# A decoder trunk on one core: the second MLP product of two chunk-layers by seven products for eight

## The chip, the cores and the metric

The kernel runs on one core of one Trainium2 chip, as one program. The metric is the device time of one execution in microseconds (us). Three runs of the kernel before took 2446.13 us in the median (2443.51 to 2448.79). TensorE multiplies matrices out of SBUF into PSUM, VectorE (DVE) and ScalarE (ACT) work on either, GpSimd (POOL) on SBUF alone, and SyncE (SP) issues most of the transfers.

## The reference

A trunk of two layers works on x, 1024 tokens by 1024 channels, in fp32. Layer 0 mixes tokens by a gated short convolution, layer 1 by sparse attention with three branches; both attend to 256 memory tokens as well, and both end with the same kind of MLP, the part that changes:

```python
x = x + jnp.concatenate([y_tok, y_mem], axis=-1) @ w_out[layer]
hm = rmsnorm(x, mlp_norm[layer])
x = x + jnp.square(jax.nn.relu(hm @ w_up[layer])) @ w_down[layer]
```

`w_up` is 1024 x 4096 and `w_down` 4096 x 1024. After layer 0 the keys and values of layer 1 are built from x.

## The kernel before

Everything is kept transposed: 128 channels on the partitions, tokens along the free dimension. The tokens are cut into two chunks c of 512 (`CH`), so there are four chunk-layers (c, l), worked in the order (0,0), (1,0), (0,1), (1,1). Attention of a chunk is woven between the MLP units of the other; (0,0) and (1,1) have none beside them, except that (0,0) carries the setup of the bias tables and the norms of its neighbours.

An fp32 product is taken as three matmuls in a rounded format (`three`, L266): both operands are split into a high part H (ScalarE copies with rounding, L263) and a low part L (VectorE subtracts, L264), and HH, HL and LH are summed in one PSUM bank. Activations are the moving operand of 512 columns, weights the stationary one of 128x128.

The MLP runs over four blocks b of 1024 hidden channels (`mlp_units`). In a block there are eight up units (`up_unit`), each giving 128 hidden channels: two weight loads of 128x512, 24 matmuls, then ReLU (ScalarE), the square (VectorE for l = 1; for l = 0 a scaling on VectorE and the square on ScalarE) and the split into H and L. Then eight down units (`down_unit`), each adding 24 matmuls to one of the eight tiles of x: one bank, and one VectorE addition of 128x512 from PSUM into x at the end (L1174). In block 3 the finished tile is also written to DRAM.

Weights come through `w_get(n)`: it splits units n to n+2 (`WB` = 3 buffers of H, of L and of the raw weights) and issues the loads of n+3 and n+4 on SP. Three PSUM banks (`mm`) are shared by these units.

The order of the program comes from two planners. The kernel's own (`Issue`) runs generators as threads against an estimated clock and so sets the order of emission: the list `plan` is the main thread, `start` adds others. The tile framework then arranges each engine's queue by its own estimate of when an instruction is ready, allots the buffers of each tag and puts in the waits; an engine works its queue strictly in that order.

Around the change: `bias_setup` starts after the first block's up units of (0,0); the norm of chunk 1 (`a_norm`) starts before the last block's up units; its scaling (`x_scale`, h at L437 and pL at L264) can begin when the last up unit has left its buffers, and the unit after the MLP (`qmem_wide`) needs all of it. `x_apart` loads chunk 1's x into the buffers of tags ks and kw for the last chunk-layer.

Of the kernel before, what the change touches and what calls it, by code (L numbers as in the profile page):

```python
# [29 lines left out]
P3 = [8, 0, 0, 0, 0, 1, 1, 0, 1, 0, 1, 1, 0, 4]  # L30
NTAIL = 6
NWARM = 2
AHEAD = 1
PACE = 2.5
LGM = 0.3
# [110 lines left out]
def trunk(ctx: ExitStack, tc: tile.TileContext, a, out):  # L146
# [7 lines left out]
    def home(tag):  # L154

        return lo if tag in ("ks", "kw", "qs", "ptH", "ptL") else sb
# [114 lines left out]

    units, dma_done, split_done = [], {}, {}

    def w_dma(n):
        if n < len(units) and n not in dma_done:
            t = sb.tile([128, 512], F32, name="wraw", tag="wraw", bufs=WB)
            if len(units[n].shape) == 3:
                DMA.dma_start(t.rearrange("p (t c) -> p t c", c=128), units[n])
            else:
                t = t[:, :units[n].shape[1]]  # L280
                DMA.dma_start(t, units[n])
            dma_done[n] = (t, iss.now + 3.5)

    def w_split(n):
        if n < len(units) and n not in split_done:
            w_dma(n)
            H = lo.tile([128, 512], F32R, name="wH", tag="wH", bufs=WB)
            L = lo.tile([128, 512], F32R, name="wL", tag="wL", bufs=WB)
            raw, t = dma_done[n]
            w = raw.shape[1]  # L290
            H, L = H[:, :w], L[:, :w]
            split(raw, H, L)
            split_done[n] = (H, L, chain(("A", ac(w)), ("V", vc(w)), at=t))

    def w_get(n, cols=128):

        for i in range(n, n + WB):
            w_split(i)
        w_dma(n + WB)
        w_dma(n + WB + 1)  # L300
        H, L, t = split_done[n]
        yield t
        return [x.rearrange("p (k c) -> p k c", c=cols) for x in (H, L)]
# [187 lines left out]
        return chain(("A", ac(256)), ("V", vc(256)))  # L491


    def bias_setup():
        tab = consts.tile([33, 12], F32, name="tab")
        DMA.dma_start(tab, a["table"])
# [2 lines left out]
        for j in range(NRV // 512):  # L499
            oh = lo.tile([33, 512], F32, name="oh", tag="ptH", bufs=PT)  # L500
            DMA.dma_start(oh, a["onehot"][:, 512 * j:512 * (j + 1)])
            yield iss.now + 4
            ohr = lo.tile([33, 512], F32R, name="ohr", tag="ptL", bufs=PT)
            ACT.activation(ohr, oh, AF.Copy)
            yield chain(("A", ac(512)))
            ps = yield from lgb.get()
            for i in range(2):
                PE.matmul(ps[:12, :], tabs[:, i], ohr, start=(i == 0), stop=(i == 1))
            iss.pe(0.43)
            rvs = sb.tile([12, 512], F32, name="rvs", tag="tmp", bufs=TM)  # L510
            ACT.activation(rvs, ps[:12, :], AF.Copy)
            lgb.put(chain(("A", ac(512))))
            DMA.dma_start(rvd[:, 512 * j:512 * (j + 1)], rvs)
        yield iss.now + 5
        for h in range(12):
            dst = skd[h][0:128 * (WP + 1)].rearrange("(p w) -> p w", w=WP + 1)[:, :WP]
# [630 lines left out]
    def up_unit(c, l, j, n):  # L1147
# [20 lines left out]
            As[:] = [None] * KT  # L1168
        yield from dense(n, Hs["m", c], evac, True)

    def down_unit(c, t, last, n):
        def evac(ps):
            x = X[c][t][0]
            V.tensor_tensor(x, ps, x, op=OP.add)  # L1174
            X[c][t][1] = chain(("V", vc(CH)))
            X[c][t][2] += 1
            if last is not None:
                DMA.dma_start(last(t), x)
            return X[c][t][1]
        yield from dense(n, As, evac)  # L1180
# [222 lines left out]
    def x_apart():  # L1403

        yield lambda: Qs[1][KT - 1] is not None
        for tag in ("ks", "kw"):
            x = home(tag).tile([128, 4, CH], F32, name="x2", tag=tag, bufs=1)
            for j in range(4):
                DMA.dma_start(x[:, j], xsd[1][len(X[1])])
                X[1].append([x[:, j], iss.now + 4, 0])  # L1410

# [10 lines left out]
    def mlp_units(c, l):  # L1422
        m = []
        for b in range(4):
            for j in range(8):
                unit(m, up_unit, c, l, j, w=[a["wu"][l, 8 * b + j]])
            last = None
            if b == 3:
                last = (lambda t: xsd[c][t]) if l == 0 else (lambda t: out[c, t])
            for t in range(8):  # L1430
                unit(m, down_unit, c, t, last, w=[a["wd"][l, b, t]])
        return m
# [132 lines left out]

    start(plan, ya, 0)
    start(plan, m_norm, 0, 0)
    plan += out_units(0, 0, x_here)
    m = mlp_units(0, 0)
    plan += m[:8]  # L1570
    start(plan, bias_setup)
    plan += m[8:-16]
    start(plan, a_norm, 1, again(lambda k: a["xT"][1, k]))
    plan += m[-16:-8]
    do(plan, lambda: p_free.add(1))
    start(plan, b_norm, 0)
    plan += m[-8:]


    unit(plan, qmem_wide, fmq[1], w=[(a["am_w"], 512)])  # L1580
# [49 lines left out]
    for fn, args, w in plan:  # L1630
        ns = []
        for x in w:
            ns.append(len(units))
            x, step = x if isinstance(x, tuple) else (x, 512)
            units += [x] if len(x.shape) == 3 else [x[:, i:i + step] for i in range(0, x.shape[1], step)]
        items.append((fn, args + tuple(ns)))

    def main():
# [111 lines left out]
```

## Time and profile before

| | |
|---|---|
| median of three runs | 2446.13 us |
| the profiled execution | 2445.52 us |
| its span, first to last instruction | 2443.8 us |
| granted TensorE clock, mean | 0.997 |
| GpSimd busy over the span | 231.7 us (9%) |
| ScalarE busy over the span | 1287.7 us (53%) |

The span begins with the first instruction; what lies between it and the execution's time is launch and end. A busy time counts the stretch in which an engine has at least one instruction in flight, so pipelined matmuls, whose records overlap, don't add up to it. A row of a group of instructions has the line, engine, operation, tiles and shape, the count, the busy time and the mean duration, and then the idle time before them and what ended it. A row of the timeline has start, duration, engine, line, operation, tiles and shape, and in brackets the idle time that came before.

### The profile page before, as it was taken

The page shows a single profiled execution, that of the slowest core. Times are in us where ns is not written, and L with a number is a line of the kernel's source. Part 1 is how long each engine was busy: PE and PEld are TensorE (multiplying, and loading weights), DVE is VectorE, ACT ScalarE, POOL GpSimd, SP SyncE. Part 2 cuts the span into 40 slices and gives each one's busy share as a digit, 9 for nine tenths or more (in the row PEclk, how much of TensorE's full clock was granted, in tenths as well). Part 3 has the DMA queues.
Part 4 walks back from the last instruction along what each step waited for, and adds up shares of the span by engine and source line. Part 5 has one row for each costly group of instructions (what it writes and reads, how often), then busy time and mean ns, then how long its engine had stood idle before and what let it go on. Part 6 is the DMA issues. An engine that isn't in the chain of part 4 may idle for free.

```text
span 2443.8 us, 35752 instructions
## 1 busy us (share of the span) xinstructions
PE 2414.5 (99%) x12062; PEld 2030.6 (83%) x12062; DVE 1508.8 (62%) x3445; ACT 1287.7 (53%) x2720; POOL 231.7 (9%) x354
## 2 busy tenths in 40 slices
PE   9999999999999999999999999999999999999999
PEld 7878788888888888888888788888888888888887
DVE  6665344464757557777746764788878874644443
ACT  5454343354645537777744553677767763423332
POOL 1120000001100132111110022200010010000000
PEclk9999999999999999999999999999999999999999
DMA  6572553445554565354265558533253244333233
GB/s 179 152 219 95 184 162 95 130 135 154 162 166 132 158 193 128 102 127 103 87 189 190 176 158 218 138 89 87 70 129 90 76 150 137 103 97 98 97 96 107
DMA packets 212791, 327.25 MB, mean 134 GB/s; under 512 B 30211, under 2 KB 79045, under 8 KB 212224
## 3 DMA queue, kind: packets, MB, share of 16 engines
q1 hardware_dynamic: 185664, 287.97, 38.5%
q0 software_dynamic: 26944, 37.00, 7.4%
q8 instruction: 95, 1.56, 0.3%
q14 instruction: 88, 0.72, 0.1%
HBM read 282.63 MB, written 46.38 MB: 135 GB/s over the span
## 4 chain that ended last, share of the span: by engine, by line
PE 85%; DMA 4%; DVE 2%; ACT 1%; issue 1%; POOL 1%; SPq 0%; ACTq 0%; DVEq 0%; POOLq 0%
PE mm L267 23%; PE mm L269 23%; PE mm L268 22%; PE pv L942 5%; PE tr L926 4%; PE lg L842 2%; PE lg L843 2%; PE lg L269 1%; PE lg L268 1%; PE lg L267 1%; DMA wraw<-in_wd_dram 1%; DMA mv<-ev 1%; DVE wL L264 1%; ACT wH L263 0%; POOL r L618 0%
## 5 line engine op out<-in xcount | busy, mean ns | idle before, releaser
L263 ACT ACTIVATE wH<-wraw 128x512 fp32r<-128x512 f32 (+2 forms) x776 | 481.6, 622 | 787.2 <-PE mm L268 594.7
L264 DVE TENSOR_TENSOR wL<-wraw,wH 128x512 fp32r<-128x512 f32 (+2 forms) x776 | 525.6, 679 | 446.0 <-ACT wH L263 433.0
L267 PE MATMUL mm<-pH,wH 128*128 128x512 f32 x1448 | 575.4, 398 | 2.6 <-DVE raw L463 2.1
L268 PE MATMUL mm<-pL,wH 128*128 128x512 f32 x1448 | 566.1, 391 | 1.0 <-DMA pL<-yd 0.8
L269 PE MATMUL mm<-pH,wL 128*128 128x512 f32 x1448 | 566.5, 391 | 0.6 <-DVE wL L264 0.4
L267 PE MATMUL mm<-qH,wH 128*128 128x512 f32 x1152 | 458.4, 398 | 2.7 <-ACT wH L263 2.7
L269 PE MATMUL mm<-qH,wL 128*128 128x512 f32 x1152 | 450.4, 391 | 1.2 <-DVE wL L264 1.1
L268 PE MATMUL mm<-qL,wH 128*128 128x512 f32 x1152 | 449.3, 390 | 0.0
L269 PEld LDWEIGHTS mm<-pH,wL 128*128 128x128 f32 x1448 | 272.6, 188 | 61.0 <-DVE wL L264 3.3
L267 PEld LDWEIGHTS mm<-pH,wH 128*128 128x128 f32 x1448 | 273.1, 189 | 57.7 <-ACT wH L263 3.5
L268 PEld LDWEIGHTS mm<-pL,wH 128*128 128x128 f32 x1448 | 273.3, 189 | 51.8 <-DMA pL<-yd 1.3
L269 PEld LDWEIGHTS mm<-qH,wL 128*128 128x128 f32 x1152 | 216.2, 188 | 50.5 <-DVE wL L264 4.1
L267 PEld LDWEIGHTS mm<-qH,wH 128*128 128x128 f32 x1152 | 216.5, 188 | 47.6 <-ACT wH L263 4.6
L268 PEld LDWEIGHTS mm<-qL,wH 128*128 128x128 f32 x1152 | 216.6, 188 | 38.6
L264 DVE TENSOR_TENSOR ptL<-tr,ptH 128x512 fp32r<-128x512 f32 (+3 forms) x284 | 175.0, 628 | 44.8 <-ACT ptH L263 42.9
L263 ACT ACTIVATE ptH<-tr 128x512 fp32r<-128x512 f32 (+3 forms) x284 | 150.8, 544 | 65.7 <-PE tr L926 57.8
L1174 DVE TENSOR_TENSOR x<-mm,x 128x512 f32<-128x512 f32 x128 | 88.2, 689 | 136.8 <-PE mm L269 136.6
L264 DVE TENSOR_TENSOR qL<-relu,qH 128x512 fp32r<-128x512 f32 x128 | 88.4, 690 | 85.6 <-ACT qH L263 85.2
L683 POOL TENSOR_TENSOR mv<-ev,mv 64x128 f32<-64x128 f32 (+1 forms) x128 | 74.8, 584 | 691.7 <-DMA mv<-ev 435.9
L854 ACT ACTIVATE ss<-ss,st 128x32 f32<-128x32 f32 (+1 forms) x192 | 105.5, 550 | 44.9 <-DVE st L848 43.2
L263 ACT ACTIVATE qH<-relu 128x512 fp32r<-128x512 f32 x128 | 80.5, 629 | 35.6 <-DVE relu L1160 34.1
L926 PE MATMUL tr<-ident,ss 128*128 128x128 f32 (+2 forms) x528 | 82.8, 277 | 0.1
(253 smaller groups left out, 3294.3 us busy)
## 6 DMA issues: line engine op xcount, KB each, us to landing
wraw<-in_wu_dram SPq DMA_DIRECT2D x256, 256.0 KB, 2.8
wraw<-in_wd_dram SPq DMA_DIRECT2D x256, 256.0 KB, 2.8
wraw<-in_a_w_dram SPq DMA_DIRECT2D x76, 256.0 KB, 3.2
wraw<-in_wo_dram SPq DMA_DIRECT2D x64, 256.0 KB, 2.7
yd<-yo SPq DMA_DIRECT2D x80, 128.0 KB, 2.9
skd<-rvd SPq DMA_DIRECT2D x12, 703.0 KB, 6.5
sw<-xsd SPq DMA_DIRECT2D x32, 256.0 KB, 3.1
wraw<-in_cw_dram SPq DMA_DIRECT2D x32, 256.0 KB, 3.0
```

Source lines behind the costliest of these rows:

```text
L263: ACT.activation(H, src, AF.Copy)
L264: V.tensor_tensor(L, src, f(H), op=OP.subtract)
L267: PE.matmul(ps, wH, xH, start=start, stop=False)
L268: PE.matmul(ps, wH, xL, start=False, stop=False)
L269: PE.matmul(ps, wL, xH, start=False, stop=stop)
L683: POOL.tensor_tensor(mv[lo:lo + 64, :w], ev[lo:lo + 64, c0:c1], mv[lo:lo + 64, :w], op=OP.add)
L842: PE.matmul(lg[:, :p1 - p0], lhs, kh[:, base + p0:base + p1], start=True, stop=False)
L843: PE.matmul(lg[:, :p1 - p0], lhs, kl[:, base + p0:base + p1], start=False, stop=True)
L854: ACT.activation(x[:, x0:x1], x[:, x0:x1], AF.Exp, bias=nm[:, hf, br, n:n + 1], scale=-1.0, accum_out=l_[:, hf, br:br + 1])
L926: PE.transpose(tr[:w, 256 * j + 128 * hf:256 * j + 128 * hf + 128], x[hf][:, o:o + w], ident)
L942: PE.matmul(pv[:, :256], v, x[:w, 256 * j:256 * j + 256], start=(gi == 1 and j == 0 and k == 0), stop=(new is None and j == len(ks) - 1 an ...
L1174: V.tensor_tensor(x, ps, x, op=OP.add)
```

## The change

For the chunk-layers in `COMBINED`, (0,0) and (1,1), the second product is taken by Strassen's algorithm in the form with 7 products and 15 additions. Two tiles of x (t, t+1), two halves of the 1024 hidden channels and two halves of the tokens (256 columns, `HT`) make a 2x2 by 2x2 block product. A `down_pair` has seven products of 4 k by 3 matmuls with 256 moving columns, each in its own bank.

The combinations of weights (S1 to S4) are made by GpSimd from the loaded tiles (`combos`, `w_combine`), in buffers of tag T of which there are two, and each of the seven is split into H and L as a unit of its own. The combinations of activations are made by VectorE in `up_combined`; the up units come in the order 0, 4, 1, 5, 2, 6, 3, 7. Of the results, three go straight into x by an addition each; four (s1, s5, s6, s7) are summed over the blocks in buffers of their own (`sums_get`, left out here: it picks the tags) and are combined into x in block 3. In block 0 ScalarE copies those four out of PSUM, later VectorE adds them.

The weights' loads are issued up to six units ahead where a unit is a combination. `bias_setup` starts before the out units of (0,0), and `x_apart` takes other buffers.

```diff
...
 P3 = [8, 0, 0, 0, 0, 1, 1, 0, 1, 0, 1, 1, 0, 4]
 NTAIL = 6
 NWARM = 2
+COMBINED = (0, 0), (1, 1)
 AHEAD = 1
 PACE = 2.5
 LGM = 0.3
...
     units, dma_done, split_done = [], {}, {}
+    class Combo:
+        def __init__(self, box, loads=(), out=None, op=None):
+            self.box, self.loads, self.out, self.op = box, loads, out, op
+    def combos(w0, w1):
+        box = {}
+        return [Combo(box, [("11", w0[:, :512])], "11"),
+                Combo(box, [("21", w1[:, :512]), ("22", w1[:, 512:])], "S1", ("21", "22", OP.add)),
+                Combo(box, [("12", w0[:, 512:])], "12"),
+                Combo(box, (), "S2", ("S1", "11", OP.subtract)),
+                Combo(box, (), "S4", ("12", "S2", OP.subtract)),
+                Combo(box, (), "S3", ("11", "21", OP.subtract)),
+                Combo(box, (), "22")]
     def w_dma(n):
         if n < len(units) and n not in dma_done:
+            u = units[n]
+            if isinstance(u, Combo):
+                for name, src in u.loads:
+                    if name[0] == "1":
+                        t = sb.tile([128, 512], F32, name="wraw", tag="wraw", bufs=WB)
+                    else:
+                        t = sb.tile([128, 512], F32, name="wr2", tag="sw", bufs=SW)
+                    DMA.dma_start(t, src)
+                    u.box[name] = (t, iss.now + 3.5)
+                dma_done[n] = None
+                return
             t = sb.tile([128, 512], F32, name="wraw", tag="wraw", bufs=WB)
-            if len(units[n].shape) == 3:
-                DMA.dma_start(t.rearrange("p (t c) -> p t c", c=128), units[n])
+            if len(u.shape) == 3:
+                DMA.dma_start(t.rearrange("p (t c) -> p t c", c=128), u)
             else:
-                t = t[:, :units[n].shape[1]]
-                DMA.dma_start(t, units[n])
+                t = t[:, :u.shape[1]]
+                DMA.dma_start(t, u)
             dma_done[n] = (t, iss.now + 3.5)
+    combined = set()
+    def w_combine(n):
+        if n < len(units) and isinstance(units[n], Combo) and units[n].op and n not in combined:
+            combined.add(n)
+            u = units[n]
+            w_dma(n)
+            x, y, op = u.op
+            (xt, t0), (yt, t1) = u.box[x], u.box[y]
+            o = sb.tile([128, 512], F32, name="wS", tag="T", bufs=2)
+            POOL.tensor_tensor(o, xt, yt, op=op)
+            u.box[u.out] = (o, chain(("P", 1.45), at=max(t0, t1)))
     def w_split(n):
         if n < len(units) and n not in split_done:
             w_dma(n)
+            w_combine(n)
             H = lo.tile([128, 512], F32R, name="wH", tag="wH", bufs=WB)
             L = lo.tile([128, 512], F32R, name="wL", tag="wL", bufs=WB)
-            raw, t = dma_done[n]
+            u = units[n]
+            raw, t = u.box[u.out] if isinstance(u, Combo) else dma_done[n]
             w = raw.shape[1]
             H, L = H[:, :w], L[:, :w]
             split(raw, H, L)
...
         for i in range(n, n + WB):
             w_split(i)
+        w_combine(n + WB)
         w_dma(n + WB)
         w_dma(n + WB + 1)
+        for i, far in ((n + WB + 2, 3), (n + WB + 3, 2)):
+            if i < len(units) and isinstance(units[i], Combo) and (far == 3 or not units[i].loads
+                                                                    or units[i].loads[0][0][0] == "2"):
+                w_dma(i)
         H, L, t = split_done[n]
         yield t
         return [x.rearrange("p (k c) -> p k c", c=cols) for x in (H, L)]
...
         DMA.dma_start(dst, f(vt))
         return chain(("A", ac(256)), ("V", vc(256)))
+    strips = set()
     def bias_setup():
         tab = consts.tile([33, 12], F32, name="tab")
...
             ACT.activation(rvs, ps[:12, :], AF.Copy)
             lgb.put(chain(("A", ac(512))))
             DMA.dma_start(rvd[:, 512 * j:512 * (j + 1)], rvs)
+        strips.add("rows")
         yield iss.now + 5
         for h in range(12):
             dst = skd[h][0:128 * (WP + 1)].rearrange("(p w) -> p w", w=WP + 1)[:, :WP]
...
             As[:] = [None] * KT
         yield from dense(n, Hs["m", c], evac, True)
+    HT = CH // 2
+    hold, Ts, t_room = {}, [None] * 4, {}
+    def up_combined(c, l, j, n):
+        k = j % 4
+        def evac(ps):
+            if l == 0:
+                yield lambda: ("m", c) in R
+            if j < 4:
+                yield lambda: not hold
+                r = hold[k] = sb.tile([128, CH], F32, name="ra", tag="vw", bufs=1)
+            else:
+                yield lambda: k in hold
+                r = tmp("relu")
+            ACT.activation(r, ps, AF.Relu)
+            free = chain(("A", ac(CH)))
+            if l == 0:
+                rs, t = R["m", c]
+                V.tensor_tensor(r, r, rs, op=OP.mult)
+                ACT.activation(r, r, AF.Square)
+                t = chain(("V", vc(CH)), ("A", ac(CH)), at=max(free, t))
+            else:
+                V.tensor_tensor(r, r, r, op=OP.mult)
+                t = chain(("V", vc(CH)), at=free)
+            if j < 4:
+                V.tensor_tensor(r[:, HT:], r[:, HT:], r[:, :HT], op=OP.subtract)
+                t = chain(("V", vc(HT)), at=t)
+            H, L = q_tile()
+            split(r, H, L)
+            As[j] = (H, L, chain(("A", ac(CH)), ("V", vc(CH)), at=t))
+            if j >= 4:
+                ra = hold[k]
+                V.tensor_tensor(ra[:, HT:], r[:, HT:], ra[:, HT:], op=OP.subtract)
+                V.tensor_tensor(ra[:, :HT], ra[:, HT:], ra[:, :HT], op=OP.subtract)
+                V.tensor_tensor(r[:, :HT], ra[:, HT:], r[:, :HT], op=OP.subtract)
+                t23 = t_room[c, l][k // 2]
+                t4 = t_room[c, l][2 + k // 2][:, k % 2]
+                H, L = t23[:, 2 * (k % 2)], t23[:, 2 * (k % 2) + 1]
+                split(ra, H, L)
+                split(r[:, :HT], t4[:, :HT], t4[:, HT:])
+                del hold[k]
+                Ts[k] = (H, L, t4, chain(("V", 3 * vc(HT)), ("A", ac(CH)), ("V", vc(CH)), ("A", ac(HT)),
+                                         ("V", vc(HT)), at=t))
+            yield 0
+            return free
+        if j == 0:
+            As[:] = [None] * KT
+            Ts[:] = [None] * 4
+            if (c, l) not in t_room:
+                t_room[c, l] = [lo.tile([128, 4, CH], F32R, name="t23", tag=x, bufs=1) for x in ("ks", "kw")]
+                t_room[c, l] += [lo.tile([128, 2, CH], F32R, name="t4", tag="qs", bufs=2) for _ in range(2)]
+        yield from dense(n, Hs["m", c], evac, True)
+    sums = {}
...
+    def down_pair(c, l, t, b, last, *ns):
+        A, B = slice(0, HT), slice(HT, CH)
+        yield lambda: len(X[c]) > t + 1
+        x0, x1 = X[c][t][0], X[c][t + 1][0]
+        if b == 0:
+            sums[t] = yield from sums_get(c, l, t)
+        s1, s5, s6, s7 = sums[t]
+        def operand(i, k):
+            if i < 2:
+                H, L, at = As[k]
+            elif i in (2, 4):
+                H, L, at = As[k + 4]
+            else:
+                H, L, t4, at = Ts[k]
+                if i == 6:
+                    return t4[:, A], t4[:, B], at
+            h = (A, B, A, B, B, A)[i]
+            return H[:, h], L[:, h], at
+        def add(to, x, y=None, op=OP.add):
+            V.tensor_tensor(to, to if y is None else y, x, op=op)
+        into = s1, s5, x0[:, A], s6, x0[:, B], s7, x1[:, A]
+        for i in range(7):
+            H, L = yield from w_get(ns[i])
+            bank = yield from mm.get()
+            ps = bank[:, :HT]
+            for k in range(4):
+                yield lambda: (As[k] if i < 2 else As[k + 4] if i in (2, 4) else Ts[k]) is not None
+                xH, xL, at = operand(i, k)
+                yield at
+                three(ps, H[:, k], L[:, k], xH, xL, k == 0, k == 3)
+                iss.pe(3 * mmc(HT))
+            if b == 0 and i in (0, 1, 3, 5):
+                ACT.activation(into[i], ps, AF.Copy)
+                free = chain(("A", ac(HT)))
+            else:
+                add(into[i], ps, op=OP.subtract if i == 6 else OP.add)
+                free = chain(("V", vc(HT)))
+            mm.put(free)
+            n = 0
+            if b == 3:
+                if i == 0:
+                    add(x0[:, A], s1)
+                    n = 1
+                elif i == 1:
+                    add(x0[:, B], s5)
+                    add(x1[:, B], s5)
+                    n = 2
+                elif i == 3:
+                    add(s6, s1)
+                    add(x0[:, B], s6)
+                    n = 2
+                elif i == 5:
+                    add(s7, s6)
+                    add(x1[:, A], s7)
+                    add(x1[:, B], s7)
+                    n = 3
+                    if l and t >= 4:
+                        raws.put()
+            if n:
+                free = chain(("V", n * vc(HT)), at=free)
+            if i in (4, 6):
+                j = t + (i == 6)
+                X[c][j][1] = free
+                X[c][j][2] += 1
+                if last is not None:
+                    DMA.dma_start(last(j), X[c][j][0])
     def down_unit(c, t, last, n):
         def evac(ps):
             x = X[c][t][0]
...
     def x_apart():
         yield lambda: Qs[1][KT - 1] is not None
-        for tag in ("ks", "kw"):
-            x = home(tag).tile([128, 4, CH], F32, name="x2", tag=tag, bufs=1)
-            for j in range(4):
+        for i in range(4):
+            if i < 3:
+                x = yield from sss.get([128, 2, CH])
+            else:
+                x = sb.tile([128, 2, CH], F32, name="x2", tag="vs", bufs=1)
+            for j in range(2):
                 DMA.dma_start(x[:, j], xsd[1][len(X[1])])
                 X[1].append([x[:, j], iss.now + 4, 0])
...
     def mlp_units(c, l):
         m = []
         for b in range(4):
-            for j in range(8):
-                unit(m, up_unit, c, l, j, w=[a["wu"][l, 8 * b + j]])
             last = None
             if b == 3:
                 last = (lambda t: xsd[c][t]) if l == 0 else (lambda t: out[c, t])
+            if (c, l) in COMBINED:
+                for j in (0, 4, 1, 5, 2, 6, 3, 7):
+                    unit(m, up_combined, c, l, j, w=[a["wu"][l, 8 * b + j]])
+                for t in range(0, 8, 2):
+                    unit(m, down_pair, c, l, t, b, last, w=combos(a["wd"][l, b, t], a["wd"][l, b, t + 1]))
+                continue
+            for j in range(8):
+                unit(m, up_unit, c, l, j, w=[a["wu"][l, 8 * b + j]])
             for t in range(8):
                 unit(m, down_unit, c, t, last, w=[a["wd"][l, b, t]])
         return m
...
     start(plan, ya, 0)
     start(plan, m_norm, 0, 0)
+    start(plan, bias_setup)
     plan += out_units(0, 0, x_here)
     m = mlp_units(0, 0)
-    plan += m[:8]
-    start(plan, bias_setup)
-    plan += m[8:-16]
+    nd = 4 if (0, 0) in COMBINED else 8
+    plan += m[:-8 - nd]
     start(plan, a_norm, 1, again(lambda k: a["xT"][1, k]))
-    plan += m[-16:-8]
+    plan += m[-8 - nd:-nd]
     do(plan, lambda: p_free.add(1))
     start(plan, b_norm, 0)
-    plan += m[-8:]
+    plan += m[-nd:]
     unit(plan, qmem_wide, fmq[1], w=[(a["am_w"], 512)])
...
         for x in w:
             ns.append(len(units))
             x, step = x if isinstance(x, tuple) else (x, 512)
-            units += [x] if len(x.shape) == 3 else [x[:, i:i + step] for i in range(0, x.shape[1], step)]
+            units += [x] if isinstance(x, Combo) or len(x.shape) == 3 else [x[:, i:i + step] for i in range(0, x.shape[1], step)]
         items.append((fn, args + tuple(ns)))
     def main():
```

## Rows read from the trace of the kernel before

**Rows 1.** Page, busy time, share of the span and instructions of each engine
```profile
PE 2414.5 (99%) x12062; PEld 2030.6 (83%) x12062; DVE 1508.8 (62%) x3445; ACT 1287.7 (53%) x2720; POOL 231.7 (9%) x354
```
**Rows 2.** Page, the chain that ended last, share of the span by engine
```profile
PE 85%; DMA 4%; DVE 2%; ACT 1%; issue 1%; POOL 1%; SPq 0%; ACTq 0%; DVEq 0%; POOLq 0%
```
**Rows 3.** Stretches of chunk-layers (0,0) and (1,1): busy time by engine, clock, DMA
```profile
core 0: us, PE busy (x) PEld busy (x) DVE busy (x) ACT busy (x) POOL busy (x), PEclk, DMA share, GB/s
210.00:516.00 306.00, 306.00 (x1354) 249.31 (x1353) 132.05 (x204) 129.71 (x222) 2.44 (x2) 1.00 0.42 133
516.00:562.00 46.00, 46.00 (x205) 38.10 (x204) 31.60 (x50) 22.63 (x37) 0.20 (x1) 1.00 0.55 172
...
2309.00:2353.00 44.00, 44.00 (x196) 36.45 (x195) 16.70 (x26) 11.60 (x19) 0.00 (x0) 1.00 0.32 99
```
**Rows 4.** Timeline of TensorE, matmuls of 512 columns: start, duration
```profile
2302.34 0.39 PE L267 MATMUL mm<-pH,wH 128*128 128x512 f32 x1
...
2304.38 0.39 PE L267 MATMUL mm<-pH,wH 128*128 128x512 f32 x1
```
**Rows 5.** Timeline of TensorE, eight matmuls of 256 columns and the next
```profile
755.55 0.28 PE L1273 MATMUL pv<-wH,FT 128*126 128x256 f32 x1
...
756.50 0.39 PE L267 MATMUL mm<-qH,wH 128*128 128x512 f32 x1
```
**Rows 6.** Timeline of the weight loads of the same matmuls
```profile
755.32 0.19 PEld L1273 LDWEIGHTS pv<-wH,FT 128*126 128x126 f32 x1
755.55 0.19 PEld L1273 LDWEIGHTS pv<-wL,FT 128*126 128x126 f32 x1
```
**Rows 7.** Timeline of VectorE, instructions back to back
```profile
56.41 0.42 DVE L264 TENSOR_TENSOR memL<-h,memH 128x256 fp32r<-128x256 f32 x1
56.74 0.68 DVE L264 TENSOR_TENSOR wL<-wraw,wH 128x512 fp32r<-128x512 f32 x1
...
2309.83 0.69 DVE L264 TENSOR_TENSOR wL<-wraw,wH 128x512 fp32r<-128x512 f32 x1 [2.03 <-ACT wH L263]
2310.44 0.68 DVE L1160 TENSOR_TENSOR relu<-relu 128x512 f32<-128x512 f32 x1
```
**Rows 8.** Timeline of GpSimd, three additions
```profile
122.97 0.74 POOL L683 TENSOR_TENSOR mv<-ev,mv 64x256 f32<-64x256 f32 x1 [3.04 <-DMA mv<-ev]
...
633.74 1.16 POOL L683 TENSOR_TENSOR mv<-ev,mv 64x256 f32<-64x256 f32 x1 [3.94 <-DVE st L746]
...
986.73 0.46 POOL L683 TENSOR_TENSOR mv<-ev,mv 64x128 f32<-64x128 f32 x1 [0.60 <-DMA mv<-ev]
```
**Rows 9.** Timeline of VectorE at the same three places
```profile
123.36 0.89 DVE L264 TENSOR_TENSOR wL<-wraw,wH 128x512 fp32r<-128x512 f32 x1 [0.98 <-ACT wH L263]
...
633.63 0.68 DVE L264 TENSOR_TENSOR wL<-wraw,wH 128x512 fp32r<-128x512 f32 x1
634.23 0.70 DVE L1056 COPY sw<-halo 128x2 f32<-128x2 f32 x1
...
986.61 0.69 DVE L1174 TENSOR_TENSOR x<-mm,x 128x512 f32<-128x512 f32 x1
```
**Rows 10.** Timeline of VectorE, chunk 1 scaled in the last stage of (0,0)
```profile
518.66 0.74 DVE L437 SCALAR_TENSOR_TENSOR h<-ss,prm,rs 128x512 f32<-128x512 f32 x1
...
535.16 0.68 DVE L264 TENSOR_TENSOR pL<-h,pH 128x512 fp32r<-128x512 f32 x1
```
**Rows 11.** Timeline of VectorE behind the last up unit of a block
```profile
2311.82 0.69 DVE L264 TENSOR_TENSOR qL<-relu,qH 128x512 fp32r<-128x512 f32 x1 [0.70 <-ACT qH L263]
```
**Rows 12.** Page, DMA issues: count, KB each, us to landing
```profile
wraw<-in_wd_dram SPq DMA_DIRECT2D x256, 256.0 KB, 2.8
```
**Rows 13.** Chain of waits, its last piece: start, duration
```profile
2439.90 0.69 DVE x L1174
```
**Rows 14.** Stretches before the out units of (0,0), columns as in rows 3
```profile
140.00:160.00 20.00, 19.21 (x86) 15.46 (x85) 11.03 (x19) 8.77 (x17) 5.09 (x8) 1.00 0.82 246
160.00:180.00 20.00, 18.74 (x84) 14.77 (x83) 11.83 (x23) 10.60 (x22) 1.67 (x1) 1.00 0.74 242
```

More of the change, by code (lines that the diff above doesn't have):

```diff
@@ new lines, in trunk, with sums_get @@
+    sums = {}
+    def sums_get(c, l, t):
+        yield lambda: "rows" in strips
+        if t < 4:
+            tag = "ptL" if t else "ptH"
+            r = [lo.tile([128, 2, HT], F32, name="sums", tag=tag, bufs=PT) for _ in range(2)]
+            return [r[0][:, 0], r[0][:, 1], r[1][:, 0], r[1][:, 1]]
+        if l == 0 and t == 6:
+            return [sb.tile([128, HT], F32, name="sums", tag=x, bufs=2) for x in ("ev", "ev", "mv", "mv")]
+        if l == 0:
+            r = sb.tile([128, 4, HT], F32, name="sums", tag="vs", bufs=1)
+        else:
+            r = (yield from raws.get()).rearrange("p a b -> p (a b)").rearrange("p (a b) -> p a b", b=HT)
+        return [r[:, i] for i in range(4)]
@@ L1405, in x_apart @@
         yield lambda: Qs[1][KT - 1] is not None
-        for tag in ("ks", "kw"):
-            x = home(tag).tile([128, 4, CH], F32, name="x2", tag=tag, bufs=1)
-            for j in range(4):
+        for i in range(4):
+            if i < 3:
+                x = yield from sss.get([128, 2, CH])
+            else:
+                x = sb.tile([128, 2, CH], F32, name="x2", tag="vs", bufs=1)
+            for j in range(2):
                 DMA.dma_start(x[:, j], xsd[1][len(X[1])])
```

## The prediction

> **What bounds the kernel now.** I read the page's busy times first: TensorE is busy 2414.5 of 2443.8 us, every other engine under two thirds [rows 1]. The chain that ended last says the same, 85% of it TensorE, 2% VectorE [rows 2]. A share over the whole span can hide a stage, so I next took the stretches of the two chunk-layers that change [rows 3]. In all of them TensorE is busy to the last hundredth at granted clock 1.00. In a plain second-product stage (2309 to 2353) VectorE works 16.7 of 44 us and GpSimd nothing. In the last such stage of chunk-layer (0,0) (516 to 562) VectorE already works 31.6 of 46 us. So work taken from TensorE shortens the time only down to the engine that is next, and that is VectorE.
>
> A matmul's busy time (0.39) overlaps the next one's; what counts is the step from start to start. At 512 columns nine steps take 2304.38 - 2302.34 = 2.04, so 0.2267 us each [rows 4]. At 256 columns, each with weights of its own, eight steps take 756.50 - 755.55 = 0.95, so 0.1188 us [rows 5].
>
> **TensorE's term.** A pair of second-product tiles is 2 x 8 x 3 = 48 matmuls of 512 columns: 48 x 0.2267 = 10.88 us. Afterwards it is 7 products x 4 x 3 = 84 matmuls of 256: 84 x 0.1188 = 9.98 us. So the eighth that the algorithm saves comes out as 0.90 of 10.88, because 256 columns cost 0.524 of 512. A stage (8 tiles, 4 pairs) is 43.5 before and 39.9 after, -3.6 us; eight stages (two chunk-layers of four blocks) give -28.8 us.
>
> The Trainium skill speaks against this term. "TensorE: Matmul & The Clock Gate", section "Measured speedup vs the span model", says that a weight load overlaps running matmuls only where it goes to another row group of the array. By that rule the 188 ns load before each full-array matmul would stand in the open, and 84 loads for 48 would make the pair 84 x (0.1188 + 0.188) = 25.8 for 48 x (0.2267 + 0.188) = 19.9 us, 32 pairs +188 us: rival (d) below. The trace says otherwise: the loads start one step ahead, while the matmul before runs, and the step stays 0.1188 [rows 5, 6]. The measurement decides.
>
> **VectorE's own work.** Back to back, its instructions start 0.61 apart at 512 columns, 0.33 at 256 [rows 7]; one that reads what the previous one wrote waits out its whole 0.42. A pair then holds 7 low-half subtractions (4 before): 7 x 0.60 = 4.2, and 7 evictions of 256 columns: 7 x 0.33 = 2.3. That is 6.5 of the pair's 9.98, less in block 0 where ScalarE takes four evictions. ScalarE, busy 11.6 of 44 in such a stage with 16 high halves [rows 3], gets 28: covered. In block 3 come 8 additions that fold the kept sums into x: 8 x 0.33 = 2.6, and about 5 of them wait on a result just written, 5 x 0.12 = 0.6. The pair is then 9.7 of 9.98: VectorE has no room left.
>
> **GpSimd's products of weights.** No row has GpSimd at 128x512. Alone it took 0.46 at 128 elements and 0.74 at 256 [rows 8], that is 0.28 per 128, so an estimate for 512 is 0.74 + 2 x 0.28 = 1.30 us. Four per pair are 5.2 of 9.98: GpSimd itself is not late, and before it had nothing to do here [rows 3]. But it collides. GpSimd ran 122.97 to 123.71 and VectorE's subtraction of two SBUF operands, begun at 123.36, took 0.89 for 0.69: it stood until 0.14 before GpSimd's end. In the other order GpSimd took 1.16 for 0.74 behind such a subtraction, and a two-column copy behind it took 0.70. An eviction with one operand in PSUM (986.61) ran beside GpSimd at its usual 0.69 [rows 8, 9]. So each weight product closes VectorE's two-operand work for about 1.1 us, in which only evictions can run. The price per product is 0 if VectorE would have been idle then, 1.1 if not; where VectorE is full I take 0.77 (one eviction of 0.33 falls inside), since subtractions and evictions alternate.
>
> **Stages that are not the last (six).** Each L subtraction has a lead: it starts when the product three back has ended and is due two products (2.85 us) later. A lead of some 1.5 us absorbs one collision, and about 0.4 per collision in a row is carried on. GpSimd's order (S4 after S1 was split, S3 after S2, and so on through two buffers) puts three in a row, 0.1 to 0.5 us lost a stage. At the start of a stage the last up unit's chain is longer. Before, its low half ends at 2312.51, 3.5 us after the stage's start at 2309 [rows 11], while the first tile needed 5.4. Now three subtractions (1.3) and two more splits follow before the fourth product's last k, due at 4.28 + 1.07 = 5.35, and the weight subtractions queue among them. I add them to about 6 us, 7 with one collision. Lost: 0 to 2 us. For both together I take 1.2 a stage, 6 x 1.2 = +7 (ends 0 and 15).
>
> **Block 3 of chunk-layer (1,1).** VectorE's sum for the stage: 28 x 0.60 = 16.8; 28 x 0.33 = 9.2; 32 x 0.33 = 10.6; 20 waits on own results 2.4; the last up unit's chain 3 x 0.60 + 4 x 0.33 and two such waits, 3.4: 42.4. Fourteen weight products fall in it (the first two run earlier): 14 x 0.77 = 10.8, so 53 if all lands on a full engine, 42 if none. Its lead at the start and end covers some 2. I take 49 between, since waits on own results and collisions partly coincide: 9 over TensorE's 39.9 (ends 1 and 13).
>
> **Block 3 of (0,0).** Here VectorE also scales chunk 1: 8 pairs of h and pL, from 518.7 to the last at 535 [rows 10], 8 x (0.66 + 0.60) = 10.1 (each 0.08 under its duration, as in [rows 7]), wanted in full by the unit that follows, and about five norm additions (3.0). 49 + 13 = 62; these fill some of the waits, so 59: 19 over 39.9 (ends 11 and 26). Before, the same work had cover: 31.6 of 46 [rows 3].
>
> **Moved and costed at nothing.** Four loads of 256 KB per pair remain, median 2.8 us to land [rows 12], and they are issued at least four products (5.7 us) ahead; without that cover each late one would show its rest. The S loads and x writes share SP's queue with wraw loads: a write that waits for a late addition holds the loads behind it, but only where VectorE is late already. The bias setup starts 16 units earlier (8 out, 8 up), nearer to the memory attention whose tiles it shares; TensorE idles 2.1 us there already [rows 14], so 0 (ends -2 and 4). x_apart takes other buffers, free once attention ends, 0 (ends 0 and 4). The very end: the last eviction is 256 wide in place of 0.69 [rows 13], -0.3.
>
> **Sum.** The profiled execution took 2445.5 us (span 2443.8), 0.6 under the median 2446.1. 2445.5 - 28.8 + 7 + 9 + 19 - 0.3 = 2451.4, so 2452 against the median: the saving is eaten by the two last blocks. Its own range is 2443 to 2464.
>
> **Rivals.** (a) Faster: the tile framework's order lets weight products fall where VectorE waits anyway. Speaks for it: VectorE is free more than half of a stage before [rows 3]; against: it has only 3% left in block 3. Then only own work counts: (1,1) +1, (0,0) 42.4 + 13 - 2 = 53.5, +13, starts +3: 2445.5 - 28.8 + 17 = 2434. It decides whether additions, not collisions, are all that fills block 3. (b) TensorE stays the bound throughout, VectorE's additions included: 2445.5 - 28.8 = 2417. It needs the scaling of chunk 1 to find room that the sum of rows does not show. (c) Slower by far: every weight product shuts VectorE out for its full 1.30 and no eviction falls inside. A pair of blocks 1 and 2 is then 7 x 0.93 + 4 x 1.30 = 11.7, above the 10.88 of before: four stages +5 each; (1,1)'s last 42.4 + 18 = 60.6, +21; (0,0)'s last 74, +34; the other starts +6: 2445.5 - 28.8 + 81 = 2498. The Trainium skill, "SBUF — State Buffer", section "Who interferes with whom", states it so: the shared port pair is held for the whole instruction and the other side fully blocks. The rows agree on the block and show 0.14 less at the end. (d) The change does not save what it says, because each weight load stands in the open at 256 columns: 2445.5 + 188 = 2634, against [rows 5].
>
> **Chances.** Forecast 0.47, (a) 0.28, (b) 0.11, (c) 0.13, (d) 0.01. The measurement can tell about 0.2% (5 us) from no change. Faster than 2441: (b) and nearly all of (a), 0.38; within 2441 to 2451: the low part of the forecast and the edge of (a), 0.18; slower: the rest of the forecast, (c) and (d), 0.44. The range takes in (b), (a) and the forecast with its upper end and leaves out most of (c): 2416 to 2474.
>
> **What would show it.** Step of the new matmuls 0.119; GpSimd 128 additions or subtractions of about 1.30; wL subtractions far over 0.69 in these stages; TensorE without idle time in blocks 0 to 2 but for about 1 us at their start; idle TensorE waiting on wL in block 3, some 9 us in (1,1), 19 in (0,0). Wrong if block 3 shows TensorE busy throughout (then a or b), or if blocks 1 and 2 last over 43.5 us (then c).

## The result, and the profile after

| | before | after |
|---|---|---|
| median beside each other, four runs each | 2447.38 us | 2483.66 us (2481.26 to 2489.42) |
| ratio, 95% interval | | 1.0154 [1.0136, 1.0171] |
| the profiled execution | 2445.52 us | 2489.42 us |

The change costs 36 us. The page after, its busy times and the shares of its chain, against [rows 1, 2]: TensorE's busy time is hardly changed, VectorE has 286 us more and holds 11% of the chain that ended last for 2%.

```profile
PE 2418.3 (97%) x13214; PEld 2077.1 (84%) x13214; DVE 1794.4 (72%) x3925; ACT 1379.4 (55%) x2912; POOL 413.1 (17%) x482
PE 81%; DVE 11%; DMA 3%; issue 2%; ACT 2%; POOL 1%; SPq 0%; DVEq 0%; ACTq 0%; POOLq 0%
```

The eight stretches of the second product, blocks 0 to 3 of (0,0) and then of (1,1), columns as in [rows 3]. A stage runs from its first matmul to the first of the next stage, the last block's to its last matmul.

```profile
258.75:301.06 42.31, 41.01 (x338) 40.47 (x337) 35.89 (x46) 24.29 (x49) 19.66 (x15) 1.00 0.34 105
344.60:388.21 43.61, 41.93 (x338) 40.72 (x336) 42.85 (x62) 19.95 (x33) 19.23 (x15) 1.00 0.30 96
431.75:479.55 47.80, 43.47 (x338) 41.11 (x336) 45.64 (x69) 22.90 (x40) 20.96 (x16) 1.00 0.42 132
524.46:589.91 65.45, 49.32 (x336) 44.47 (x335) 64.64 (x111) 27.29 (x47) 22.81 (x18) 0.95 0.34 106
2170.40:2212.35 41.95, 41.22 (x337) 40.52 (x336) 36.23 (x46) 23.85 (x48) 20.47 (x15) 1.00 0.33 103
2255.90:2300.16 44.26, 42.47 (x337) 40.87 (x336) 43.62 (x62) 19.52 (x32) 19.51 (x15) 1.00 0.29 95
2343.71:2387.96 44.25, 42.45 (x338) 40.86 (x336) 43.61 (x62) 19.53 (x32) 19.49 (x15) 1.00 0.30 95
2431.51:2482.72 51.21, 45.34 (x337) 41.48 (x335) 50.34 (x90) 17.89 (x30) 19.22 (x14) 1.00 0.22 77
```

Each took 43.3 to 43.5 before, block 0 of (0,0) 48.9 with the bias setup's 14 matmuls in it. Only the two first blocks gain. In the plain blocks 1 and 2 of (1,1) VectorE is busy 43.6 of 44.3 us: it has become the bound there too, not only in the last blocks. The up stages last as before.

One pair's piece of block 1 of (1,1) shows why. First VectorE, then GpSimd, then TensorE's third part of that product and its first step after (L265 is the subtraction that makes a low half, L1321 here an eviction, that is an addition out of PSUM, L325 a combination of weights, called a product of weights from here on):

```profile
2264.69 0.68 DVE L265 TENSOR_TENSOR wL<-wS,wH 128x512 fp32r<-128x512 f32 x1
2265.29 0.41 DVE L1321 TENSOR_TENSOR sums<-sums,mm 128x256 f32<-128x256 f32 x1
2265.63 1.72 DVE L265 TENSOR_TENSOR wL<-wr,wH 128x512 fp32r<-128x512 f32 x1
2267.27 0.41 DVE L1321 TENSOR_TENSOR ss<-ss,mm 128x256 f32<-128x256 f32 x1
...
2265.50 1.30 POOL L325 TENSOR_TENSOR wS<-wS,wraw 128x512 f32<-128x512 f32 x1 [1.34 <-DVE wL L265]
...
2265.65 0.28 PE L268 MATMUL mm<-t,wH 128*128 128x256 f32 x1
...
2266.84 0.28 PE L269 MATMUL mm<-t,wH 128*128 128x256 f32 x1
2267.41 0.39 PE L270 MATMUL mm<-t,wL 128*128 128x256 f32 x1 [0.28 <-DVE wL L265]
```

GpSimd is released by the low half before it (end 2265.37) and starts 0.13 later. By then VectorE has already begun its eviction; what comes next is a subtraction, which stands until 0.13 before GpSimd's end and then needs its 0.68. It took 1.72: 1.04 us lost, with no eviction inside, and TensorE waits for the result. I call a stretch in which GpSimd keeps VectorE from such work a closure. Ten matmuls of 256 columns start in 2266.84 - 2265.65 = 1.19 us, 0.119 each, weight loads hidden.

Over that stage (groups: count, busy time, mean ns) the 28 low halves of weights take 31.4 us for 19.3 at their 0.69, and two subtractions of 256 columns 1.5 each for 0.41:

```profile
L265 DVE TENSOR_TENSOR wL<-wS,wH 128x512 fp32r<-128x512 f32 x15 | 16.3, 1086 | 0.0
L265 DVE TENSOR_TENSOR wL<-wraw,wH 128x512 fp32r<-128x512 f32 x9 | 9.3, 1029 | 1.4 <-ACT wH L264 1.4
L265 DVE TENSOR_TENSOR wL<-wr,wH 128x512 fp32r<-128x512 f32 x4 | 5.8, 1462 | 0.0
L1262 DVE TENSOR_TENSOR ra<-ra 128x256 f32<-128x256 f32 x1 | 1.5, 1512 | 0.0
L265 DVE TENSOR_TENSOR t<-relu,t 128x256 fp32r<-128x256 f32 x1 | 1.5, 1511 | 0.0
```

That is 14.3 us more for the 14 products of the stage. One by one they cost 0.98 to 1.10; none fell where VectorE was idle. Nor is it that the products come late: before the low halves of the combinations (wS) VectorE has no idle time.

### The profile page after: what moved, and what is told of

It reads as the page before. It is cut to its first block, busy times and chain, and to the rows that moved or that the text cites. A ratio compares the mean times of both kernels' runs of the same rounds, so it can differ in the third digit from the quotient of the medians.

```text
span 2487.3 us, 39205 instructions
## 1 busy us (share of the span) xinstructions
PE 2418.3 (97%) x13214; PEld 2077.1 (84%) x13214; DVE 1794.4 (72%) x3925; ACT 1379.4 (55%) x2912; POOL 413.1 (17%) x482
## 4 chain that ended last, share of the span: by engine, by line
PE 81%; DVE 11%; DMA 3%; issue 2%; ACT 2%; POOL 1%; SPq 0%; DVEq 0%; ACTq 0%; POOLq 0%
PE mm L268 21%; PE mm L270 21%; PE mm L269 21%; PE pv L996 5%; DVE wL L265 5%; PE tr L980 4%; PE lg L896 2%; PE lg L897 2%; DMA mv<-ev 1%; PE lg L269 1%; PE lg L270 1%; PE lg L268 1%; DVE sums L1321 1%; DMA wraw<-in_wd_dram 1%; ACT wH L264 1%
## 5 line engine op out<-in xcount | busy, mean ns | idle before, releaser
L264 ACT ACTIVATE wH<-wraw 128x512 fp32r<-128x512 f32 (+2 forms) x712 | 440.8, 621 | 578.8 <-PE mm L269 388.1
L265 DVE TENSOR_TENSOR wL<-wraw,wH 128x512 fp32r<-128x512 f32 (+2 forms) x712 | 506.3, 712 | 316.8 <-ACT wH L264 304.6
L268 PE MATMUL mm<-qH,wH 128*128 128x512 f32 (+1 forms) x1152 | 405.7, 352 | 7.8 <-DVE sums L1321 2.5
L270 PE MATMUL mm<-qH,wL 128*128 128x512 f32 (+1 forms) x1152 | 398.5, 346 | 6.3 <-DVE wL L265 6.0
L269 PE MATMUL mm<-qL,wH 128*128 128x512 f32 (+1 forms) x1152 | 395.6, 344 | 2.6 <-DVE qL L265 2.6
L265 DVE TENSOR_TENSOR ptL<-tr,ptH 128x512 fp32r<-128x512 f32 (+3 forms) x284 | 175.0, 628 | 44.1 <-ACT ptH L264 42.3
L264 ACT ACTIVATE wH<-wS 128x512 fp32r<-128x512 f32 x128 | 80.6, 631 | 117.7 <-POOL wS L325 62.9
L265 DVE TENSOR_TENSOR wL<-wS,wH 128x512 fp32r<-128x512 f32 x128 | 125.7, 982 | 9.0 <-ACT wH L264 8.3
L268 PE MATMUL mm<-t,wH 128*128 128x256 f32 x384 | 110.6, 288 | 11.9 <-DVE sums L1321 3.8
L270 PE MATMUL mm<-t,wL 128*128 128x256 f32 x384 | 113.4, 295 | 7.6 <-DVE wL L265 7.1
```

Of the source, the lines that this page charges most:

```text
L264: ACT.activation(H, src, AF.Copy)
L265: V.tensor_tensor(L, src, f(H), op=OP.subtract)
L268: PE.matmul(ps, wH, xH, start=start, stop=False)
L269: PE.matmul(ps, wH, xL, start=False, stop=False)
L270: PE.matmul(ps, wL, xH, start=False, stop=stop)
```

## The experiments

All are edits of the changed kernel, but for one of the kernel before. The runs without products, without last additions and with GpSimd only writing leave a part of the computation out, and so measure time alone. Stages in us; ratios to runs of the kernel before made beside each (medians 2442 to 2447 us), with 95% intervals.

| run | us | ratio | (0,0) blocks 0 to 3 | (1,1) blocks 0 to 3 |
|---|---|---|---|---|
| the change | 2483.66 | 1.0154 | 42.3 43.6 47.8 65.5 | 42.0 44.3 44.3 51.2 |
| no products on GpSimd | 2438.42 | 0.9972 [0.9959, 0.9985] | 40.7 40.6 41.1 52.6 | 40.4 40.5 40.5 41.2 |
| products on VectorE | 2455.36 | 1.0045 [1.0026, 1.0063] | 40.7 41.2 41.8 60.1 | 40.7 41.2 41.2 47.6 |
| no last additions | 2465.89 | 1.0080 [1.0064, 1.0097] | 42.6 43.6 48.2 57.7 | 42.0 44.3 44.2 44.1 |
| neither | 2433.53 | 0.9953 [0.9939, 0.9968] | 40.7 40.6 41.1 51.1 | 40.4 40.5 40.5 40.4 |
| neither, scaling spread | 2427.07 | 0.9938 [0.9913, 0.9962] | 40.7 40.6 41.1 43.9 | 40.4 40.5 40.5 40.4 |
| change, scaling spread | 2488.37 (one) | | 42.3 43.6 47.8 64.6 | 42.0 44.2 44.3 51.5 |
| GpSimd only writes | 2439.75 (one) | | 40.8 40.7 41.1 52.6 | 40.4 40.5 40.5 41.2 |
| (1,1) only | 2453.67 | 1.0042 [1.0027, 1.0058] | as before, block 0 43.5 | 42.0 44.2 44.3 51.5 |
| plain block 3, products on VectorE | 2428.89 | 0.9941 [0.9926, 0.9956] | 40.7 41.2 41.8 43.3 | 40.7 41.2 41.2 43.3 |
| plain block 3, products on GpSimd | 2455.61 | 1.0048 [1.0032, 1.0064] | 42.6 44.0 49.6 43.3 | 42.0 44.2 48.7 43.3 |
| before, bias setup moved | 2444.35 | 0.9999 [0.9989, 1.0009] | as before, block 0 43.5 | as before |

**No products on GpSimd.**

```diff
-            o = sb.tile([128, 512], F32, name="wS", tag="T", bufs=2)
-            POOL.tensor_tensor(o, xt, yt, op=op)
-            u.box[u.out] = (o, chain(("P", 1.45), at=max(t0, t1)))
+            u.box[u.out] = (xt, max(t0, t1))
```

> GpSimd's four weight products per pair are left out (the first operand is used in their place). Theory P (shared port: each product shuts out VectorE's two-operand subtraction for about 1.04 us, and VectorE is the bound of blocks 1 to 3): 112 of 128 collisions go, blocks 1 and 2 fall from 44.3 to about 40.5 us in (1,1), the last blocks from 51 and 65 to about 43 and 56, the time from 2484 to about 2450; wL with a mean near 0.69. Theory W (VectorE is full of its own additions and subtractions, the collisions coincide with waits): 2475 to 2480, blocks 1 and 2 stay near 44.

45 us come back, more than I expected, and every stage but (0,0)'s last is TensorE's own. Its stretches, block 3 of (0,0), then block 1 and block 3 of (1,1):

```profile
512.86:565.45 52.59, 46.91 (x336) 44.93 (x335) 50.68 (x110) 26.67 (x46) 2.09 (x4) 0.90 0.40 124
2224.34:2264.70 40.36, 40.36 (x337) 40.24 (x335) 32.80 (x62) 19.51 (x32) 0.00 (x0) 1.00 0.33 107
2392.39:2433.58 41.19, 40.94 (x337) 40.40 (x335) 39.28 (x91) 18.24 (x30) 0.00 (x0) 1.00 0.30 102
```

With the same 62 instructions as after, VectorE is busy 32.8 us for 43.6. The 10.8 between are less than the 14.3 of the closures, because an instruction with a gap behind it counts its whole 0.69 as busy and a packed one its step of 0.61. And with all additions in block 3 it works 39.3 of 41.2: the additions alone fit.

**Products on VectorE.**

```diff
-            POOL.tensor_tensor(o, xt, yt, op=op)
+            V.tensor_tensor(o, xt, yt, op=op)
```

> The four products per pair move from GpSimd to VectorE, 0.60 each back to back in place of 1.04 of closed port. Theory P: VectorE's sum for blocks 1 and 2 is 16.8 + 9.2 + 3.4 + 9.6 = 39, under TensorE's 40: both at 40.5 to 41.5; last blocks 49 and 62; time about 2468. Theory W (own work is what counts): every product adds 0.60 to a full VectorE, 128 x 0.60 = 77 less what was lost in collisions before: 2484 or slower.

28 us faster than with the idle engine doing them, and 13 less than I had put down. A product costs VectorE 0.69 us as its own instruction, 0.61 back to back [rows 7], against 1.04 as GpSimd's. The four groups of block 1 of (1,1), 14 in all:

```profile
L325 DVE TENSOR_TENSOR wS<-wraw,wr 128x512 f32<-128x512 f32 x4 | 2.7, 686 | 0.0
L325 DVE TENSOR_TENSOR wS<-wr,wr 128x512 f32<-128x512 f32 x4 | 2.7, 685 | 0.0
L325 DVE TENSOR_TENSOR wS<-wraw,wS 128x512 f32<-128x512 f32 x3 | 2.1, 686 | 0.0
L325 DVE TENSOR_TENSOR wS<-wS,wraw 128x512 f32<-128x512 f32 x3 | 2.1, 685 | 0.0
```

**No last additions**, and **neither** (this and the first edit together).

```diff
-            if b == 3:
-                if i == 0:
-                    add(x0[:, A], s1)
...
+            if b == 3 and i == 5 and l and t >= 4:
+                raws.put()
```

> The eight additions per pair that fold the kept sums into x in block 3 are left out. Theory P: block 3 becomes like block 2: 44.3 for 51.2 in (1,1), about 56 for 65.5 in (0,0), time about 2467. Theory W (additions are the whole loss): -27 or more, 2455.

> Both left out: GpSimd's products and the additions of block 3. Theory P and W alike: seven of the eight stages bound by TensorE at 40 to 41 us, the last of (0,0) by the scaling of chunk 1 beside it, about 45; time 2422 to 2430. If it stays above 2440 there is a third cause: the start of the stages, the moved bias setup or the middle of the program.

The first came out as expected. With the second, block 3 of (1,1) shows how little the causes add up: alone the additions cost 0.8 us over 40.4, the products 3.7, both 10.8. So behaves a sum on VectorE that passes TensorE's by a little with the products and by much with both. But the time was above the 2422 to 2430 that I expected, and (0,0)'s last stage still took 51.1 for 45, so a third cause was missing. Its VectorE there, and TensorE's clock in stretches of 4 us:

```profile
520.63 0.68 DVE L265 TENSOR_TENSOR wL<-wraw,wH 128x512 fp32r<-128x512 f32 x1
521.24 2.07 DVE L486 SCALAR_TENSOR_TENSOR h<-ss,prm,rs 128x512 f32<-128x512 f32 x3
523.23 2.05 DVE L265 TENSOR_TENSOR pL<-h,pH 128x512 fp32r<-128x512 f32 x3
525.19 0.41 DVE L1319 TENSOR_TENSOR sums<-sums,mm 128x256 f32<-128x256 f32 x1
...
524.00:528.00 4.00, 2.25 (x10) 2.24 (x11) 4.00 (x8) 1.10 (x2) 0.00 (x0) 0.69 0.15 33
528.00:532.00 4.00, 3.76 (x28) 3.55 (x27) 2.91 (x6) 2.57 (x5) 0.00 (x0) 0.88 0.47 158
532.00:536.00 4.00, 1.18 (x7) 1.00 (x8) 4.00 (x8) 2.04 (x4) 0.00 (x0) 0.97 0.14 53
536.00:540.00 4.00, 4.00 (x24) 4.00 (x24) 2.94 (x7) 0.98 (x2) 0.00 (x0) 0.60 0.63 218
```

Three h and three pL of chunk 1 stand in a row ahead of an eviction; TensorE waits 3 us for it, twice, and behind each wait the granted clock falls to 0.69 and 0.60 of 2.4 GHz, that is mostly the lower of its levels.

**The scaling of chunk 1 spread**, first with neither products nor additions, then in the whole change.

```diff
-        yield from x_scale(("a", c), xs, ("a", c), C_MIXG, p_tile)
+        yield from x_scale(("a", c), xs, ("a", c), C_MIXG, p_tile, pace=4.0)
```

> The kernel without GpSimd products and without the additions of the last blocks (both left out of the computation, as in the run that gave 2433.53 us), with one edit more: the scaling of chunk 1 is paced at 4 us a block, so that its h and pL parts no longer stand three by three in VectorE's queue in the last stage of (0,0). My theory (the third cause of the loss is these bursts, about 4 us of VectorE in a row ahead of evictions, and the clock that falls to 0.60 to 0.97 behind the waits): that stage goes from 51.1 us to 41 to 43, the granted clock there stays at 1.00, and the time is 2423 to 2427 us. Rival (the sum of VectorE's work of that stage is the cause, whatever its order): the stage stays at 49 to 51 us and the time at 2431 to 2434. Second rival (only the clock, which falls for another reason): the waits on VectorE go, but the clock still falls below 0.9, and the stage is 45 to 48 us.

> The changed kernel, whole, with the scaling of chunk 1 paced at 4 us a block as in the run before (which took the last stage of (0,0) from 51.1 to 43.9 us without products and additions). My theory: in the changed kernel VectorE works 64.64 of the 65.45 us of that stage, so it is bound by the sum of VectorE's work, closures by GpSimd included, and the order matters little: the stage stays at 62 to 65.5 us, though the clock may come back from 0.95 to 1.00, and the time stays at 2478 to 2487 us. Rival (the bursts cost there what they cost without products): the stage falls by about 7 us to 58, and the time to some 2477.

The last stage of (0,0) in the first and in the second run:

```profile
512.90:557.00 44.10, 43.20 (x337) 41.29 (x336) 42.11 (x84) 27.40 (x48) 2.09 (x4) 1.00 0.49 156
...
526.02:590.61 64.59, 47.87 (x337) 42.76 (x336) 64.41 (x111) 27.68 (x47) 24.94 (x18) 0.97 0.34 107
```

Without products the bursts and the clock behind them were worth 7.2 us (43.9 for 51.1, clock 1.00), a little less than I expected, since VectorE's 42.1 us now stand there. In the whole change the order is worth 0.9: VectorE is busy 64.4 of 64.6 us whatever the order. The time itself, one run, is a little above what I had put down for my theory and not below the change's.

**GpSimd only writes.**

```diff
-            POOL.tensor_tensor(o, xt, yt, op=op)
+            POOL.memset(o, 0.0)
```

> The changed kernel with each GpSimd product of the combinations replaced by a GpSimd memset of the same tile (the weight combinations are left out of the computation; GpSimd writes the tile and reads nothing). If what shuts VectorE's subtraction out is that GpSimd reads two SBUF operands while VectorE does too, the subtraction wL takes its 0.68 us again for nearly all of the 14 pairs of a stage, and blocks 1 and 2 last 40.4 to 41.3 us, as with no GpSimd product. If any GpSimd instruction shuts it out for its own length, wL shows 0.68 us plus the length of the memset less 0.2 to 0.3, and the blocks stay at 41.5 us or more unless the memset is far shorter than 1.3 us.

Every stage is as with nothing on GpSimd. VectorE, then GpSimd, in block 1 of (1,1):

```profile
2230.12 0.68 DVE L265 TENSOR_TENSOR t<-ra,t 128x512 fp32r<-128x512 f32 x1
2232.33 0.68 DVE L265 TENSOR_TENSOR wL<-wr,wH 128x512 fp32r<-128x512 f32 x1
...
2230.26 0.52 POOL L325 MEMSET wS<- 128x512 f32 x1 [1.68 <-DVE wL L265]
2232.13 0.53 POOL L325 MEMSET wS<- 128x512 f32 x1 [1.35 <-DVE wL L265]
```

The memsets run beside subtractions of two SBUF operands, and those take their 0.68. So GpSimd's being at work does not shut them out; what the memset lacks, beside 0.8 us of length, is the reading. The Trainium skill, "SBUF — State Buffer", section "Who interferes with whom", has it so: a VectorE instruction with two inputs in SBUF contends with a GpSimd instruction that reads SBUF, and not with one that only writes. The runs agree: 1.72 us beside a product, 0.68 beside a memset.

**(1,1) only.**

```diff
-COMBINED = (0, 0), (1, 1)
+COMBINED = (1, 1),
```

> The change kept in chunk-layer (1,1) alone, products on GpSimd. By the stages of the changed kernel's trace (42.0, 44.3, 44.3, 51.2 for 4 x 43.5): +8 us, and 0 to 3 for the bias setup, which still starts early: 2452 to 2455. The other 28 to 30 us of the loss then belong to (0,0).

As expected: its four stages sum to 8 us more than the 173.8 of before, the rest of the 36 us comes with (0,0).

**Plain block 3**, the kept sums folded into x by a thread of their own beside block 3's up units; products on VectorE, then on GpSimd.

```diff
+    def fold_sums(c, l):
...
+                V.tensor_tensor(to, to, x, op=OP.add)
...
-            if (c, l) in COMBINED:
+            if (c, l) in COMBINED and b == 3:
+                start(m, fold_sums, c, l)
+            elif (c, l) in COMBINED:
```

> Seven products in blocks 0 to 2 alone, with the weight products on VectorE; block 3 is taken plainly, with the eight products' eight units, and the kept sums are folded into x by VectorE during its up units, where it has room. Theory P with the full last block: six stages at 40.7 to 41.8 for 43.5 (as in the run with the products on VectorE), 14 us gained; the last blocks as before; the bias setup's move 0 to 3: about 2432 beside 2444 for the kernel before. If folding or the move costs as much as is gained (theory N, the start of stages and the moved setup eat it): 2444 or more.

> The same with the weight products on GpSimd, as in the changed kernel. Theory P: the six stages as measured there, 42.3, 43.6, 47.8, 42.0, 44.3, 44.3 us, together 3 above the plain ones: about 2449. Theory W (the last block's additions are the loss): 2432, like the run with the products on VectorE.

The first leaves nothing out and beats both kernels, the one before by 16.6 us in the medians (11 to 18 by the interval). Six stages sum to 247.0 us for 6 x 43.52 = 261.1, and the last blocks cost what they did before. The second missed by 7 us: of the fold's 32 additions 25 and 27 land in block 2's second product (49.6 and 48.7 us), where GpSimd leaves no room. With the products on VectorE only 7 land there, and that stage takes 41.8 and 41.2. The order that the planners make thus differs between the two, beside the engine of the products.

**The kernel before with the bias setup moved** ahead of the out units.

```diff
+    start(plan, bias_setup)
     plan += out_units(0, 0, x_here)
...
-    start(plan, bias_setup)
```

> The kernel before with the bias setup alone started before the out units. Costed at nothing in the forecast; the changed kernel's trace has its out units 2 to 4 us late, so 0 to +4: 2444 to 2448. If it is a cause of its own: +5 or more.

No cost within 0.1%: the 14 matmuls leave block 0 and stand before the MLP instead.

## Why the prediction was wrong

The direction was right, the size was not: 2484 for 2452, outside the range. In the profiled execution the change took 43.9 us more where I had 5.9. Stage by stage, over what I had put down: the two block 0 +2.1 us, the three plain blocks 1 and 2 +8.8, block 2 of (0,0) +6.7, block 3 of (0,0) +6.5 and of (1,1) +2.2, TensorE's saving taken as forecast in each; in all 26. The stretch from (0,0)'s last stage to (1,1)'s first, whose program is hardly changed, was 8.3 us longer in this execution (1580.5 for 1572.2 us; 1567 to 1580 over the runs here). Of that 6.1 is idle time of TensorE (23.9 for 17.8) and 2.2 busy time, at a mean granted clock of 0.99 for 1.00. The start was 1.8 longer. The causes of both stay open, and the median lies 5.8 below this execution.

- **TensorE's term**: right in kind. The step is 0.119 as worked out and the loads stay hidden, so rival (d) is out. (The rule behind (d) stands in the Trainium skill's "TensorE: Matmul & The Clock Gate" under "The mechanism", not under the section that the prediction names.) A stage without VectorE's load takes 40.4 to 40.7, not 39.9: the eight save some 24 us and not 28.8.
- **GpSimd 1.30 each**: measured 1.30 in the median. **The block on two-operand work**, freed 0.14 early: measured 0.13. **The bias setup at 0**: measured 0.
- **"I take 0.77 (one eviction of 0.33 falls inside), since subtractions and evictions alternate"**: the mis-sized term. The alternation is there, but GpSimd mostly starts right behind a low half, with an eviction already under way, so that the next instruction, a subtraction, meets the closure: 1.04, for all 14 products of each of the plain blocks 1 and 2 of (1,1).
- **"A lead of some 1.5 us absorbs one collision", 1.2 a stage**: this failed with it. I counted leads where a sum was due. VectorE's own 16.8 + 9.2 + 3.4 = 29.4 and 14 x 0.77 = 10.8 make 40.2, which would just have fitted; with 14 x 1.04 = 14.6 they make 44.0, and the stages took 43.6 to 44.3. A lead delays, it doesn't make room in a full engine. My own test, blocks 1 and 2 over 43.5, came out for rival (c): its mechanism was the nearer one, its 1.30 too much by the 0.26 in which the two overlap. (Its sum was short as well: 4 x 11.7 = 46.8 is 6.9 over 39.9, where it put 5.)
- **Block 3 of (1,1), 49, and of (0,0), 59**: I had summed 53.2 and 66.2, and then took off 4 and 7 for waits that would coincide. They took 51.2 and 65.5. Where VectorE is busy 98 to 99%, next to nothing coincides: its busy time without products, 39.3 and 50.7, and the closures, 12.3 and 14.0 as the excess of its instructions' durations, make 51.6 and 64.7. That my two sums came near is in part luck: own work of 42.4 and 55.4 was 3 to 5 too much, closures of 10.8 too little. The stages without products were rival (a)'s: 40.9 and 53.5 by its terms, 41.2 and 52.6 measured, the second by luck too, since there the clock stood at 0.90, which (a) did not have. So additions and scaling alone do not make the change lose, though (0,0)'s last stage keeps 9 us of them; the products do, with 45 of the 50 us by which the change stands above the run with neither.
- **Block 2 of (0,0)** was not listed: the norm of chunk 1 is started before the last block's up units, and the framework put seven of its additions into this stage, where two of them meet closures too (in the mean 0.98 us for 0.68). With no products the same 69 instructions cost nothing (41.1):

```profile
L416 DVE TENSOR_TENSOR raw<-raw,sq 128x512 f32<-128x512 f32 x7 | 6.8, 977 | 0.0
```

## What to carry to other kernels

Before an element-wise operation on two SBUF tiles goes to an idle GpSimd, charge it to VectorE where that engine works on two SBUF tiles as well: here 1.04 us for each, against 0.61 if VectorE did it itself. When work is traded from the bound engine to another, sum the other engine's slots stage by stage, with every closure and all other work of the stage in it, and set that beside the bound; leads and coincidences count only while the sum leaves room. And keep the trade where the sum fits: with the combinations on VectorE, three blocks of four by seven products gained 17 us, and the fourth lost more than that (60.1 and 47.6 us for 43.3 each).

## What was not expected of the hardware

A GpSimd memset, which only writes SBUF (0.53 us), cost VectorE's subtractions nothing here, an instruction that reads two tiles (1.30 us) cost them 1.04. And behind two waits of TensorE of 3 us each the granted clock fell, to means of 0.69 and 0.60 in stretches of 4 us, so that bursts of six VectorE instructions, some 4 us each time, cost 7.2 us of a stage in which VectorE had work for 44 of 51.
